# The last projection of a hybrid linear-attention layer: gate folded into the weights, partial products added into the rows, engine order pinned

## The chip, the core and the metric

The kernel runs on one NeuronCore of a Trainium2 chip. Five engines work in parallel, each through its own queue in order: PE (TensorE, matmuls; its weight loads are listed as PEld), DVE (VectorE), ACT (ScalarE), POOL (GpSimd) and SP (SyncE, which here only issues DMAs). An engine waits at the head of its queue until the semaphores that its next instruction names are set, and everything queued behind that instruction waits with it. 16 DMA engines carry the transfers between DRAM and on-chip memory (SBUF). Matmuls write to PSUM, a small accumulation memory.

The metric is the device time of one execution in microseconds, as the median of several runs.

## The reference, cut to what matters

One layer normalises the latent rows, runs two linear-attention mixers over them, merges the two with sigmoid gates, projects with `w_o`, multiplies by a residual gate `gt_x` (one value for each of 1024 columns), adds the input rows and applies a final RMSNorm. The change touches what is computed by these lines:

```
merged = gates[..., :D_MODEL] * jnp.matmul(ya, w_gla_out) + gates[..., D_MODEL:] * jnp.matmul(yb, w_gdn_out)
out_x = jnp.matmul(merged, w_o)                       # 2048 rows x 1024, w_o 1024 x 1024
x = x + (gt_x[:, None, :] * out_x).astype(dtype)
return rmsnorm(x, final_g)                            # x * rsqrt(mean(x*x) + 1e-6) * g, row by row
```

All is float32. The kernel gets that accuracy by splitting each operand into a rounded half (`hi`) and a remainder (`lo`), and multiplying hi by hi, hi by lo and lo by hi.

## The kernel before

Up to about 1770 us of the profile the kernel projects the inputs and runs the two mixers; none of that changes. Then comes its last part, in two stages.

**Merge** (`out_merge`, four calls with g = 0 to 3, each for 512 rows). For each of 8 column tiles j and both mixers i there are 12 matmuls of 128x512 into one PSUM bank (L1597): i = 0 into `pm` (two banks), i = 1 into `pz` for g > 0 (three banks). DVE multiplies each bank by its gate tile `ga` (L1600), adds the two (L1604), and SP writes the sum to the DRAM tensor `d_m` (L1605). Gate tiles are loaded by SP (L1592) into three buffers for i = 0, which come free when the write to `d_m` has landed, and four for i = 1.

**Projection** (`phase_out`, the loop at L1711 to L1776, eight blocks of 256 rows). One level of Strassen's scheme in Winograd's form: a block's input is cut into A11, A12, A21, A22, sums S1 to S4 are formed (`m_sums`, L1643), and seven products p = 0 to 6 (`PRODUCTS`) are taken with seven blocks of weights of 512x512: B11, B21, B22 are cuts of `w_o`, and T1 to T4 are differences of cuts. Each product is 12 matmuls (L1737). Products 0, 2, 4 and 6 add up in one PSUM bank, 1 and 5 in a second, 3 has a third. Partial sums that are needed twice are copied out by ACT (L1742, products 0, 1, 2, 4). DVE or POOL add what is missing (L1751, L1754, L1757), `fin` multiplies by the gate row `gtb` on DVE (L1724), adds into the row tile `x` on POOL (L1725; on DVE at the very end), and ACT squares the result with a row sum (L1726). `flush` takes the reciprocal root on POOL (L1703, then `rsqrt`, L155 and L156), scales the rows on DVE (L1707) and SP writes them out (L1709).

Weights are cut and split by `wo_block`: DMA loads from `w_o` (L1612), differences on DVE (L1624, L1629), `split` (ACT L132 for the rounded half, DVE or POOL L135 for the remainder). B11 and T1 are made ahead of merge 3, T2, B21 and T3 inside it, B22 and T4 inside the first block of the projection. The inputs of a product are split by `m_halves`, through the same two lines, remainders by turns on DVE and POOL.

The order on each engine is chosen by a scheduler from the order of the program and its own estimates of durations; `keep_in_program_order` pins an instruction to its place in program order among those that are pinned. Before, only L1707 in this part is pinned. SP's order comes from the same scheduler.

Of the kernel before, what the change touches and what calls it, by code (L numbers as in the profile page):

```python
# [97 lines left out]
class Build:  # L98
# [1333 lines left out]
    def phase_mix(self):  # L1432
# [4 lines left out]
        self.d_m = dp.tile([NLAT // 2, P, 8, 256], F32, name="dm")  # L1437
        self.d_o = [[dp.tile([P, 512], F32, name=f"do{i}_{l}") for l in range(NLAT)] for i in range(2)]
# [144 lines left out]
    def out_merge(self, g):  # L1583
# [3 lines left out]
        pair = lambda t: t.rearrange("p (e t) -> p e t", e=2)  # L1587
        for j in range(8):
            gs = []
            for i in range(2):  # L1590
# [9 lines left out]
                nc.vector.scalar_tensor_tensor(ga, ga, 1.0, ps, op0=ALU.add, op1=ALU.mult)  # L1600
# [3 lines left out]
            nc.vector.tensor_tensor(gs[0], gs[0], gs[1], op=ALU.add)  # L1604
# [3 lines left out]
    def wo_piece(self, kh, ch, e):  # L1608
        t = self.w_raw().rearrange("p (k n) -> p k n", k=2)
        r0 = (4 * kh + 2 * e) * P  # L1610
        src = self.io["w_o"][0, r0:r0 + 2 * P, 512 * ch:512 * ch + 512]
        self.nc.sync.dma_start(t, src.rearrange("(k p) n -> p k n", p=P))  # L1612
        return t

    def wo_block(self, name, hi, lo):
        nc = self.nc
        for e in range(2):
            ks = slice(2 * e, 2 * e + 2)
            if name[0] == "B":
                x = self.wo_piece(int(name[1]) - 1, int(name[2]) - 1, e)  # L1620
            elif name in ("T1", "T3"):
                a, b = ((0, 1), (0, 0)) if name == "T1" else ((1, 1), (0, 1))
                x, y = self.wo_piece(*a, e), self.wo_piece(*b, e)
                nc.vector.tensor_tensor(x, x, y, op=ALU.subtract)  # L1624
            else:
                o = self.wo["T1" if name == "T2" else "T2"]
                x = self.wo_piece(1, 1 if name == "T2" else 0, e)
                for t in o:
                    nc.vector.tensor_tensor(x, x, t[:, ks].bitcast(F32), op=ALU.subtract)  # L1629
            self.split(hi[:, ks], lo[:, ks], x, lo=self.LO[e])  # L1630
        self.wo[name] = (hi, lo)
# [9 lines left out]
    def m_sum(self, w, nm, a, b, op):  # L1641
        w[nm] = w[b] if nm == "S4" else self.mp.tile([P, 4, P], F32, name="r0" if nm in ("S1", "S3") else "r1", bufs=1)
        self.nc.vector.tensor_tensor(w[nm], w[a], w[b], op=op)  # L1643
# [9 lines left out]
    def m_halves(self, w, p):  # L1653
        hi, lo = (self.mp.tile([P, 4, P], F32R, name=n, bufs=self.NHL) for n in ("hi", "lo"))
        self.split(hi, lo, w[PRODUCTS[p][0]], lo=self.LO[p % 2])
        w[p] = (hi, lo)

    NHL = 4

    def phase_out(self):  # L1660
        nc, io = self.nc, self.io
        with ExitStack() as ctx:
            self.mctx.close()
            fp = self.pool("of", 1, ctx=ctx)
            fg = fp.tile([P, D], F32, name="fgb")
            gtb = fp.tile([P, D], F32, name="gtb")
            nc.sync.dma_start(gtb, self.d_gt[0:1, :].broadcast_to([P, D]))
            nc.sync.dma_start(fg, io["final_g"].unsqueeze(0).broadcast_to([P, D]))
            xp = self.pool("ox", 3, ctx=ctx)
            self.mp = self.pool("om", 1, ctx=ctx)  # L1670
            self.yp = self.pool("oy1", 1, ctx=ctx)
            self.sp = self.pool("og", 4, ctx=ctx)
            self.out_y(1)
            self.wo = {}
            yt = lambda pool, i: [pool.tile([P, 4, 512], F32R, name=f"y{2 * i + x}") for x in range(2)]
            order = [b for g in self.groups for b in g]
            for g in range(1, 4):
                gen = self.out_merge(g)
                if g < 3:
                    y = self.y2  # L1680
                    self.out_y(g + 1)
                    nxt, self.y2 = self.y2, y
                    for _ in gen:
                        pass
                    self.y2 = nxt
                    continue
                self.wo_block("B11", *yt(self.bp, 0))
                self.wo_block("T1", *yt(self.bp, 1))
                for n, _ in enumerate(gen):
                    if n in (3, 7, 11):  # L1690
                        self.wo_block({3: "T2", 7: "B21", 11: "T3"}[n], self.w_blk(), self.w_blk())
            w = self.m_raws(order[0])
            self.m_sums(w, 0)
            for p in range(3):
                self.m_halves(w, p)
            self.m_sums(w, 1)
            pend = []
            pm = self.pool("opp", 3, PSUM, ctx=ctx)

            def flush(parts=1):  # L1700
                while pend:
                    l, x, ss = pend.pop()
                    nc.gpsimd.tensor_tensor(ss[:, 0:1], ss[:, 0:1], ss[:, 1:2], op=ALU.add)  # L1703
                    rs = self.rsqrt(xp, ss[:, 0:1], 1.0 / D, 1, nc.gpsimd)
                    for i in range(parts):
                        cs = slice(i * (D // parts), (i + 1) * (D // parts))
                        self.tc.keep_in_program_order(nc.vector.scalar_tensor_tensor(  # L1707
                            x[:, cs], x[:, cs], rs, fg[:, cs], op0=ALU.mult, op1=ALU.mult))
                        nc.sync.dma_start(self.out[0, l * P:(l + 1) * P, cs], x[:, cs])  # L1709

            for bi, b in enumerate(order):  # L1711
                end = bi + 1 == len(order)
                nw = None if end else self.m_raws(order[bi + 1])
                xs = []
                for i in range(2):
                    x = xp.tile([P, D], F32, name="x")
                    nc.sync.dma_start(x, io["x"][0, (2 * b + i) * P:(2 * b + i + 1) * P, :])
                    xs.append((x, xp.tile([P, 2], F32, name=f"oss{i}")))
                tile_ = lambda: self.sp.tile([P, 512], F32, name="ga")

                def fin(s, src, i, h, last=False):
                    x, ss = xs[i]
                    cs = slice(512 * h, 512 * h + 512)
                    nc.vector.tensor_tensor(s, src, gtb[:, cs], op=ALU.mult)  # L1724
                    (nc.vector if last else nc.gpsimd).tensor_tensor(x[:, cs], x[:, cs], s, op=ALU.add)  # L1725
                    nc.scalar.activation(s, x[:, cs], AF.Square, accum_out=ss[:, h:h + 1])  # L1726

                for p, (_, r) in enumerate(PRODUCTS):
                    if p in (0, 1, 3):
                        ps = pm.tile([P, 512], F32, name="pp") if bi % 2 else self.pv()  # L1730
                        a, c = (ps if p == 0 else a), (ps if p == 1 else None if p == 0 else c)
# [8 lines left out]
                    if p in (0, 1, 2, 4):  # L1740
                        s = tile_()
                        nc.scalar.copy(s, ps)  # L1742
                    if p == 0:
                        s1 = s
                        flush()
                    elif p == 1:
                        s5 = s
                    elif p == 2:
                        s2 = s
                    elif p == 3:  # L1750
# [61 lines left out]
```

## Time and profile before

| | us |
|---|---|
| Median of 3 runs | 2187.87 (2186.38 to 2188.19) |
| The profiled execution | 2195.01 |
| Its span, first to last instruction | 2192.9 |

The page's first part gives each engine's busy time: PE leads with 94% of the span, DVE has 58%, ACT 42%, POOL 41%. That is an average over all stages. The change lies in the last 350 us, so what follows is read from windows of that stretch, from the waits there, from the chain of work that ended last, and from the instructions in order of time. In such a row the first number is the start in us from the start of the span, the second the time in us, then engine, line, operation, output tile, input tiles, and in brackets how long the engine was idle before and what ended the idle time.

### The profile page before, as it was taken

What the parts mean: (1) busy time and instruction counts of PE and PEld (TensorE: products, weight loads), DVE (VectorE), ACT (ScalarE), POOL (GpSimd) and SP (SyncE); (2) the same over time, 40 slices, a digit from 0 to 9 for tenths busy, and PEclk for the clock granted to TensorE, in tenths of its full rate; (3) what the DMA queues carried; (4) which work ended last, traced back from release to release, by engine and by line L of the source; (5) the groups of instructions that cost most, each with busy time, mean ns of one, the idle gap of its engine ahead of it and who ended that gap; (6) DMA issues with size and microseconds to landing.
All of it is one profiled execution on the core that took longest, in us unless ns stands there. A gap on an engine that the chain in (4) does not pass through costs nothing.

```text
span 2192.9 us, 40261 instructions
## 1 busy us (share of the span) xinstructions
PE 2063.7 (94%) x15208; PEld 1690.1 (77%) x15208; DVE 1280.7 (58%) x2188; ACT 926.7 (42%) x2240; POOL 903.7 (41%) x807
## 2 busy tenths in 40 slices
PE   5999999999999999999999999998989889998896
PEld 2688888888888888777777777788878877876675
DVE  3813555567776554555555555666677765467564
ACT  3654255555542223443444443455555551013332
POOL 2410122222320106665666662656566552025554
PEclk7999999999999999999999999999998989999998
DMA  7323122222222224443444444888898877773432
GB/s 278 108 87 115 55 60 64 66 63 61 68 73 75 83 81 144 132 143 118 140 155 136 154 136 150 280 290 304 271 303 278 272 215 243 239 228 130 163 106 87
DMA packets 289758, 337.52 MB, mean 154 GB/s; under 512 B 23208, under 2 KB 215964, under 8 KB 289564
## 3 DMA queue, kind: packets, MB, share of 16 engines
q1 hardware_dynamic: 289564, 334.94, 47.0%
q8 instruction: 120, 1.97, 0.4%
q14 instruction: 74, 0.61, 0.1%
HBM read 216.63 MB, written 118.23 MB: 153 GB/s over the span
## 4 chain that ended last, share of the span: by engine, by line
PE 72%; DVE 8%; DMA 7%; ACT 5%; POOL 4%; issue 3%; SPq 1%; DVEq 0%; POOLq 0%; ACTq 0%
PE pz L371 45%; PE pm L1597 3%; PE pz L1597 2%; PE pp L1737 2%; PE pz L1737 2%; DMA g<-dg 1%; PE pe L936 1%; DMA wr<-in_w_o 1%; PE pl L988 1%; PE pl L995 1%; PE pe L1118 1%; PE pz L1080 1%; PE pl L996 1%; DMA ga<-dgate 1%; POOL x L1725 1%
## 5 line engine op out<-in xcount | busy, mean ns | idle before, releaser
L371 PE MATMUL pz<-hi,wh 128*128 128x512 f32 (+1 forms) x1560 | 621.6, 399 | 0.9 <-DVE hi L134 0.8
L371 PE MATMUL pz<-lo,wh 128*128 128x512 f32 (+1 forms) x1560 | 600.5, 385 | 1.8 <-POOL lo L135 1.8
L371 PE MATMUL pz<-hi,wl 128*128 128x512 f32 (+1 forms) x1520 | 588.6, 387 | 0.0
L371 PEld LDWEIGHTS pz<-lo,wh 128*128 128x128 f32 x1560 | 294.7, 189 | 51.1 <-POOL lo L135 3.6
L371 PEld LDWEIGHTS pz<-hi,wh 128*128 128x128 f32 x1560 | 294.5, 189 | 47.1 <-DVE hi L134 1.6
L371 PEld LDWEIGHTS pz<-hi,wl 128*128 128x128 f32 x1520 | 286.2, 188 | 53.6 <-issue 0.4
L135 POOL TENSOR_TENSOR wl<-w,wh 128x1024 fp32r<-128x1024 f32 x44 | 110.9, 2520 | 435.3 <-ACT wh L132 291.0
L569 DVE SCALAR_TENSOR_TENSOR acc<-zpad,cw,acc 128x1024 f32<-128x1024 f32 x192 | 269.9, 1406 | 6.6
L873 DVE CAST_PREDICATED U<-kit,pl 128x256 f16<-128x256 int32 x216 | 91.1, 431 | 138.2 <-PE pl L996 134.4
L989 ACT CAST ppb<-pl 128x256 f16<-128x256 f32 x216 | 73.5, 373 | 166.8 <-PE pl L988 155.7
L1597 PE MATMUL pm<-y,wb 128*128 128x512 f32 x480 | 119.8, 402 | 8.5 <-DVE ga L1600 6.2
L1216 POOL TENSOR_TENSOR E<-E,ak 128x256 f32<-128x256 f32 x96 | 79.0, 843 | 112.2 <-ACT E L1209 65.2
L1597 PEld LDWEIGHTS pm<-y,wb 128*128 128x128 f32 x480 | 91.9, 193 | 30.7 <-DVE ga L1600 6.0
L135 DVE TENSOR_TENSOR sql<-sq,sqh 128x512 fp32r<-128x512 f32 (+1 forms) x36 | 28.0, 805 | 140.1 <-ACT sqh L132 139.9
L624 POOL TENSOR_TENSOR acc<-acc,sq 128x512 f32<-128x512 f32 x32 | 51.4, 1614 | 137.5 <-ACT sq L623 89.7
L554 ACT COPY zpad<-pz 128x512 f32<-128x512 f32 x48 | 28.2, 587 | 137.6 <-PE pz L371 137.6
L1118 PE MATMUL pe<-wt,gh 128*128 128x256 f32 x264 | 76.2, 316 | 9.4 <-ACT E L1209 4.4
L135 POOL TENSOR_TENSOR y<-wr,y 128x1024 fp32r<-128x1024 f32 x11 | 30.2, 2752 | 120.2 <-ACT y L132 120.2
L132 ACT CAST y<-wr 128x1024 fp32r<-128x1024 f32 x22 | 22.4, 1045 | 130.1 <-PE pm L1597 102.6
L873 DVE CAST_PREDICATED Tm<-kit,pl 128x256 f16<-128x256 int32 x180 | 76.2, 423 | 0.0
L995 PEld LDWEIGHTS <-Tm 128*128 128x128 f16 x864 | 55.1, 98 | 26.4 <-issue 21.9
L132 ACT CAST wh<-w 128x1024 fp32r<-128x1024 f32 x44 | 46.2, 1049 | 68.2 <-PE pz L371 56.0
(329 smaller groups left out, 4474.8 us busy)
## 6 DMA issues: line engine op xcount, KB each, us to landing
dgate<-ob SPq DMA_DIRECT2D x96, 256.0 KB, 2.1
gd<-dgd SPq DMA_DIRECT2D x32, 768.0 KB, 9.0
w<-in_w_in SPq DMA_DIRECT2D x44, 512.0 KB, 3.6
qk<-dqkv SPq DMA_DIRECT2D x32, 512.0 KB, 6.1
ga<-dgate SPq DMA_DIRECT2D x64, 256.0 KB, 3.4
x<-in_x SPq DMA_DIRECT2D x28, 512.0 KB, 5.0
dqkv<-acc SPq DMA_DIRECT2D x192, 64.0 KB, 1.6
dgd<-tm SPq DMA_DIRECT2D x36, 256.0 KB, 3.4
```

Of the source, the lines that this page charges most:

```text
L132: nc.scalar.copy(dst_hi, src)
L135: getattr(nc, lo).tensor_tensor(dst_lo, src, dst_hi.bitcast(F32), op=ALU.subtract)
L371: nc.tensor.matmul(ps[:, 0:n], a[:, kk, :], b[:, kk, :], start=(k == 0), stop=(k == last - 1))
L569: nc.vector.scalar_tensor_tensor(acc, src, wcol, acc, op0=ALU.mult, op1=ALU.add)
L624: nc.gpsimd.tensor_tensor(v, v, r, op=ALU.mult)
L873: self.nc.vector.copy_predicated(out, mv, data)
L989: nc.scalar.copy(ppl, pc.rearrange("p h (j i) -> p h j i", i=m))
L995: nc.tensor.matmul(pu[:, h], Tm[:, h], ppl[:, h], start=True, stop=True)
L1118: self.nc.tensor.matmul(out, g[:, i, ct * P:(ct + 1) * P], self.wt[:, d, cols[0]:cols[1]], start=(j == 0), stop=(j == 1))
L1216: nc.gpsimd.tensor_tensor(E[:, :, li, 1], E[:, :, li, 1], k, op=ALU.mult)
L1597: nc.tensor.matmul(ps, self.wab[j // 2][wi][:, 4 * i + k, (j % 2) * P:(j % 2) * P + P], yy[:, k, :], start=(n == 0), stop=(n == 11))
L1737: nc.tensor.matmul(ps, w[p][u][:, kk, :], self.wo[r][v][:, kk, :], start=(k == 0 and p in (0, 1, 3)), stop=(k == 11), skip_group_check=True)
```

## The change

Five edits, all in the last part.

1. **Weights ahead, with the gate in them.** `w_o` is no longer cut for each block. In merges 1 and 2 a generator `prep(k)` (k = 0 to 3, two in each merge) loads two row tiles of `w_o` of 128x1024, multiplies both by `gtb` on DVE (L1670), forms T1 to T4 by four subtractions of 128x512 on DVE (L1661) and writes seven pieces of 256 KB to seven new DRAM tensors `d_wo`. In merge 3 a generator `blocks()` loads the finished blocks from there (L1693, 512 KB each) and splits them (L1699, L1700).
2. **No copies, no gate multiply.** After each product DVE adds the PSUM bank straight to half a row tile, `x += ps` (L1823). Which half follows from `ACC`; a bank that goes on accumulating is read once for each partial sum. L1742, L1751, L1754, L1757, L1724 and L1725 are gone.
3. **Splits.** The rounded half stays on ACT (`m_hi`, L1632, five buffers, one product further ahead than before), the remainder is always on DVE (`m_lo`, L1637, four buffers).
4. **Square, root and scaling** are placed by hand: the square (L1772) one product behind the addition, the root after products 0 and 6, the two scalings (L1785) after products 1 and 2 of the next block.
5. **Order and buffers.** All DVE, ACT and POOL instructions of this part but those of `split` are pinned; the rows of the next block are loaded from product 3 on; row tiles have four buffers (three before), gate tiles for i = 1 three (four before).

```
+        self.d_wo = {r: dp.tile([P, 4, 512], F32, name=f"dwo{r}") for _, r in PRODUCTS}
...
+        pin = self.tc.keep_in_program_order if g else lambda x: x
...
+            def prep(k):
+                a, b = self.w_raw(), self.w_raw()
+                for t, r in ((a, k), (b, k + 4)):
+                    nc.sync.dma_start(t, io["w_o"][0, r * P:r * P + P, :])
+                yield
+                yield
+                for t in (a, b):
+                    pin(nc.vector.tensor_tensor(t, t, gtb, op=ALU.mult))
+                    yield
+                nc.sync.dma_start(self.d_wo["B11"][:, k], a[:, lo_])
...
+                sub(t1, a[:, hi_], a[:, lo_])
+                nc.sync.dma_start(self.d_wo["T1"][:, k], t1)
...
+            def place(nm, raw, e, dst, eng):
+                hi, lo = self.wo[nm] = dst
+                ks = slice(2 * e, 2 * e + 2)
+                pin(nc.scalar.copy(hi[:, ks], raw[e]))
+                pin(eng.tensor_tensor(lo[:, ks], raw[e], hi[:, ks].bitcast(F32), op=ALU.subtract))
...
+                for _ in gen:
+                    next(work, None)
...
+            ACC = ((0, 0), (1, 1), (0, 1), (0, 0), (1, 1), (0, 1), (1, 0))
...
-                    if p in (0, 1, 2, 4):
-                        s = tile_()
-                        nc.scalar.copy(s, ps)
...
+                    square()
+                    i, h = ACC[p]
+                    x, ss = xs[i]
+                    cs = slice(512 * h, 512 * h + 512)
+                    pin(nc.vector.tensor_tensor(x[:, cs], x[:, cs], ps, op=ALU.add))
+                    if p > 2:
+                        sq.append((x, ss, h))
+                    if p in (0, 6):
+                        root()
+                    if p < 4:
+                        self.m_lo(w, p + 3)
+                    elif nw is not None:
+                        self.m_lo(nw, p - 4)
+                    if nw is not None and p == 3:
+                        self.m_sums(nw, 0)
+                    if p < 3:
+                        self.m_hi(w, p + 4)
+                    elif nw is not None:
+                        self.m_hi(nw, p - 3)
...
+                    if p in (1, 2):
+                        flush()
```

How the instructions move is shown at three places. In these rows `x` is a row tile, `pp` and `pz` are PSUM banks of a product, `lo` and `hi` the two halves of a split, `r` a sum S1 to S4, `wr` a raw load.

ACT in the projection, where one block ends and the next begins. Before:

```order
L1726 ACTIVATE ga,oss_23106<-x 128x512
L132 CAST hi<-r_23262 128x512
L1742 COPY ga<-pp 128x512
L132 CAST hi<-r_23198 128x512
L1742 COPY ga<-pp 128x512
L132 CAST hi<-wr 128x512
L1742 COPY ga<-pp 128x512
```

And now, at the same place:

```order
L1772 ACTIVATE ga,oss<-x 128x512
L1632 CAST hi<-r_23064 128x512
L1772 ACTIVATE ga,oss<-x 128x512
L1632 CAST hi<-wr 128x512
L1772 ACTIVATE ga,oss<-x 128x512
L1632 CAST hi<-r_23135 128x512
L1632 CAST hi<-r_23064 128x512
```

The copies of PSUM banks, which stood behind the previous block's squares, are gone from ACT.

DVE in the projection, about a block's worth of its queue before:

```order
L1707 SCALAR_TENSOR_TENSOR x<-x,rsq,fgb 128x1024 x2
L135 TENSOR_TENSOR lo<-r_23094,hi 128x512
L1643 TENSOR_TENSOR r_23196<-wr 128x512
L1643 TENSOR_TENSOR r_23198<-r_23196,wr 128x512
L135 TENSOR_TENSOR lo<-wr,hi 128x512
L1751 TENSOR_TENSOR ga<-pz,ga 128x512
L135 TENSOR_TENSOR lo<-wr,hi 128x512
L1724 TENSOR_TENSOR ga<-ga,gtb 128x512 x2
L1643 TENSOR_TENSOR r_23262<-wr,r_23198 128x512
L1757 TENSOR_TENSOR ga<-pz,ga 128x512
```

And now, products 0 to 4 of a block:

```order
L1823 TENSOR_TENSOR x<-x,pp 128x512
L1637 TENSOR_TENSOR lo<-wr,hi 128x512
L1823 TENSOR_TENSOR x<-x,pp 128x512
L1637 TENSOR_TENSOR lo<-r_23294,hi 128x512
L1785 SCALAR_TENSOR_TENSOR x<-x,rsq,fgb 128x1024
L1823 TENSOR_TENSOR x<-x,pp 128x512
L1637 TENSOR_TENSOR lo<-r_23223,hi 128x512
L1785 SCALAR_TENSOR_TENSOR x<-x,rsq,fgb 128x1024
L1823 TENSOR_TENSOR x<-x,pp 128x512
L1637 TENSOR_TENSOR lo<-wr,hi 128x512
L1620 TENSOR_TENSOR r_23380<-wr 128x512
L1620 TENSOR_TENSOR r_23382<-r_23380,wr 128x512
```

Each product now has one addition from its bank, one remainder, and at most one larger task on DVE.

SP in merge 2, where before there were only gate loads (`ga<-dgate`), writes of merged tiles (`dm<-ga`) and a few early loads. It now reads:

```order
L1677 DMA dwoT_14758<-r_21920 128x512
L1679 DMA dwoT_14761<-wr 128x512
L1607 DMA dm<-ga 128x2x256
L1682 DMA dwoT_14759<-r_21921 128x512
L1594 DMA ga<-dgate 128x2x256
L1666 DMA wr<-in_w_o 128x1024
L1594 DMA ga<-dgate 128x2x256 x2
L1607 DMA dm<-ga 128x2x256
L1687 DMA dwoT_14763<-r_21980 128x512
L1594 DMA ga<-dgate 128x2x256 x3
L1693 DMA wr<-dwoB_14757 128x1024
```

The writes to `d_wo` (L1672 to L1687) and the loads of `w_o` (L1666) stand between the gate loads that the merge waits for.

More of the change, by code (lines that the diff above doesn't have):

```diff
@@ L1603, in out_merge @@
                     yield
-            nc.vector.tensor_tensor(gs[0], gs[0], gs[1], op=ALU.add)
+            pin(nc.vector.tensor_tensor(gs[0], gs[0], gs[1], op=ALU.add))
             nc.sync.dma_start(self.d_m[bs, :, j, :].rearrange("b p t -> p b t"), pair(gs[0]))
             yield
[L1608 to L1631, printed above, removed]
     def m_raws(self, b):
@@ L1682, in phase_out @@
                     nxt, self.y2 = self.y2, y
[L1683 to L1698, printed above, removed]
+                    work = itertools.chain(prep(2 * g - 2), prep(2 * g - 1))
+                else:
+                    nxt, work = None, blocks()
+                for _ in gen:
+                    next(work, None)
+                for _ in work:
+                    pass
+                self.y2 = nxt
@@ new lines, in phase_out, with square, root @@
+            w = self.m0
+            sq, done, pend = [], [], []
+            def square():
+                for x, ss, h in sq:
+                    junk = self.sp.tile([P, 512], F32, name="ga")
+                    pin(nc.scalar.activation(junk, x[:, 512 * h:512 * h + 512], AF.Square, accum_out=ss[:, h:h + 1]))
+                sq.clear()
+            def root():
+                for l, x, ss in done:
+                    pin(nc.gpsimd.tensor_tensor(ss[:, 0:1], ss[:, 0:1], ss[:, 1:2], op=ALU.add))
+                    pend.append((l, x, self.rsqrt(xp, ss[:, 0:1], 1.0 / D, 1, nc.gpsimd)))
+                done.clear()
@@ L1711, in phase_out @@
+            nxs = load_x(order[0])
             for bi, b in enumerate(order):
                 end = bi + 1 == len(order)
+                xs = nxs
                 nw = None if end else self.m_raws(order[bi + 1])
[L1714 to L1718, printed above, removed]
@@ new lines, in phase_out @@
+                    if nw is not None and p == 3:
[4 more added lines that the diff above has]
+                        self.m_hi(nw, p - 3)
+                    if nw is not None and p == 6:
+                        self.m_sums(nw, 1)
+                    if p in (1, 2):
+                        flush()
+                    if p == 3 and not end:
+                        nxs = load_x(order[bi + 1])
@@ L1775, in phase_out @@
+                    if bi == 0 and p < 4:
+                        if p % 2 == 0:
+                            d = yt(self.yp, 0) if p else wt()
+                        place(("B22", "T4")[p // 2], self.late[p // 2], p % 2, d, nc.gpsimd)
+                    if p == 5:
+                        done.append((2 * b, *xs[0]))
+                    elif p == 6:
+                        done.append((2 * b + 1, *xs[1]))
                 w = nw
+            flush()
+            square()
+            root()
```

159 lines of the change are left out of this document (101 added, 58 removed).

## The prediction

> **What bounds the kernel now.** I read the busy time of the engines in windows first, then PE's waits from 1925 us on, then the chain of work and the instructions in order of time.
>
> ```profile
> 1800.00:1900.00 100.00, 95.36 (x417) 77.27 (x416) 48.86 (x61) 19.87 (x51) 22.63 (x11) 0.98 0.79 253
> 1900.00:2000.00 100.00, 92.83 (x389) 74.72 (x388) 62.93 (x69) 18.12 (x23) 21.18 (x9) 0.97 0.66 203
> 2000.00:2100.00 100.00, 85.74 (x329) 66.32 (x328) 65.14 (x69) 36.04 (x77) 59.33 (x57) 0.91 0.37 131
> 2100.00:2193.00 93.00, 73.32 (x294) 57.45 (x292) 48.85 (x58) 29.50 (x66) 47.04 (x52) 0.90 0.29 103
> ```
>
> Columns: window, length, busy PE, PEld, DVE, ACT, POOL, granted PE clock, share of the DMA engines, GB/s. The merges (to 1979) keep PE busy; the projection, from there on, does not, at a lower clock, and there the DMA engines are idle two thirds of the time. What PE waits for:
>
> ```profile
> PE pp L1737 <- ACT ga L1742: 10.5, 5, 3.2
> PE pz L1737 <- ACT ga L1742: 9.3, 4, 3.2
> PE pz L1737 <- ACT y L132: 3.9, 1, 3.9
> PE pz L1737 <- DVE ga L1600: 2.9, 1, 2.9
> PE pm L1597 <- DVE ga L1600: 2.3, 2, 1.5
> PE pz L1737 <- POOL y L135: 0.7, 1, 0.7
> ```
>
> Total us, times, longest. The rows of L1737 sum to 27.3 us: 19.8 for ACT's copies, 7.5 where merge turns into projection. How large the stage is, and how fast its matmuls can go:
>
> ```profile
> 1979.43 0.63 PE L1737 MATMUL pz<-y,hi 128*128 128x512 f32 x2
> ...
> 2033.76 1.16 PE L1737 MATMUL pp<-y,hi 128*128 128x512 f32 x2 [1.89 <-ACT ga L1742]
> 2034.71 0.63 PE L1737 MATMUL pp<-y,lo 128*128 128x512 f32 x1
> ...
> 2035.99 0.63 PE L1737 MATMUL pp<-y,lo 128*128 128x512 f32 x1
> ...
> 2046.37 0.63 PE L1737 MATMUL pz<-wb,hi 128*128 128x512 f32 x2
> ...
> 2056.17 0.63 PE L1737 MATMUL pz<-wb,hi 128*128 128x512 f32 x2
> ...
> 2181.04 0.39 PE L1737 MATMUL pp<-y,lo 128*128 128x512 f32 x1
> ```
>
> The first row begins the projection, the last ends it: 2181.43 - 1979.43 = 202.0 us. From 2046.37 to 2056.17 lie 14 groups of three matmuls: 0.70 us a group, 2.80 a product, 19.6 a block. 8 blocks are 156.8 us. So 45.2 us are lost: 27.3 in waits, 17.9 in slow matmuls. The rows at 2034.71 and 2035.99 show those: after the wait of 1.89 us a group takes 1.28 us, not 0.70. Why PE waits for a copy of 0.57 us:
>
> ```profile
> 2082.02 1.30 POOL ga L1754
> 2083.34 1.76 DVE ga L1724
> 2086.30 1.10 DVE lo L135
> 2088.09 1.67 POOL x L1725
> 2089.75 0.80 issue
> 2090.78 1.23 POOL x L1725
> 2093.80 7.42 PE pz L1737 x24
> ```
>
> In the chain, product 2 of a block starts (2093.80) when ACT has copied product 0; the copy stands behind the squares of the block before, these behind POOL's additions (L1725), these behind DVE's gate multiply. The waits for `ga` above count nine of these for eight blocks: about one a block.
>
> **The change: the projection.** A bank is now read by one DVE addition. The nearest rows:
>
> ```profile
> L1751 DVE TENSOR_TENSOR ga<-pz,ga 128x512 f32<-128x512 f32 x3 | 2.1, 688 | 1.8 <-PE pz L1737 1.8
> L135 DVE TENSOR_TENSOR lo<-wr,hi 128x512 fp32r<-128x512 f32 x10 | 6.8, 683 | 0.0
> L1643 DVE TENSOR_TENSOR r<-wr,r 128x512 f32<-128x512 f32 x11 | 7.5, 678 | 0.0
> L1707 DVE SCALAR_TENSOR_TENSOR x<-x,rsq,fgb 128x1024 f32<-128x1024 f32 (+1 forms) x17 | 27.3, 1643 | 37.8 <-POOL rsq L156 37.8
> L132 ACT CAST hi<-r 128x512 fp32r<-128x512 f32 x22 | 13.3, 614 | 1.2 <-PE pz L1737 0.8 <-PE pp L1737 0.4
> L1726 ACT ACTIVATE ga<-x 128x512 f32<-128x512 f32 x23 | 14.6, 633 | 57.4 <-POOL x L1725 57.4
> 2184.47 1.28 DVE L1707 SCALAR_TENSOR_TENSOR x<-x,rsq,fgb 128x1024 f32<-128x1024 f32 x1 [2.24 <-POOL rsq L156]
> ```
>
> DVE in a block: 7 additions x 0.69 + 7 remainders x 0.68 + 4 sums x 0.68 + 2 scalings x 1.28 = 14.9 us (15.6 at the mean of 1.64), under 19.6. The fullest products hold 0.69 + 0.68 + 2 x 0.68 = 2.73 or 0.69 + 0.68 + 1.28 = 2.65, under 2.80, and a bank is wanted again only one product later, so DVE may run 2.1 us late before PE feels it. ACT: 7 x 0.61 and 4 squares of 0.82 (0.63 and 0.19 to read the sum) are 7.6. POOL keeps small roots. Each remainder is made two products ahead; the root of a row is asked for at least one product ahead of its scaling; in SP's queue the second half of a block's input, though behind two writes of rows, is issued a whole block ahead. I find no steady wait: 8 x 19.6 = 156.8.
>
> I allow 3.3 us for the first block. The remainder for its product 1 comes after the last merge additions (1.0), POOL's splits of B22 and T4 hold up DVE's sums before product 6 (0.7), and one wait slows the matmuls (three groups x 0.58 = 1.7, rounded down to 1.6). Bounds: 0 to 7.5, today's whole loss at this place.
>
> **The tail.**
>
> ```profile
> 2185.67 0.69 DVE x L1725
> 2186.36 0.02 issue
> ...
> 2188.38 0.75 DVE x L1707
> ```
>
> Today PE's last matmul is followed by 2192.9 - 2181.43 = 11.5 us. The last addition starts only at 2185.67, behind a gate multiply and a scaling; from its end 2.0 us pass to the last scaling, and 4.5 from there to the end. Now the addition starts 0.1 after PE: 0.1 + 0.7 + 2.0 + 4.5 = 7.3; 7.5 with a wait for the other row's scaling. Gain 4.0.
>
> **The merges pay for it.**
>
> ```profile
> DMA packets 16830, 20.32 MB, mean 242 GB/s; under 512 B 1014, under 2 KB 14393, under 8 KB 16825
> q1 hardware_dynamic: 16825, 20.26, 77.3%
> ...
> 1800.00:1810.00 10.00, 10.00 (x46) 8.29 (x45) 3.91 (x6) 7.50 (x36) 5.54 (x4) 1.00 0.94 294
> ...
> 1882.41 0.69 DVE L1600 SCALAR_TENSOR_TENSOR ga<-ga,pm 128x512 f32<-128x512 f32 x1 [2.75 <-DMA ga<-dgate]
> ```
>
> The first two rows are of 1848 to 1932, merges 1 and 2: 242 GB/s at 77.3% share, so 313 at a full one. The third is the highest share of any 10 us window here, 0.94 at 294 GB/s. From SP's order I count in these two merges 27 writes of 0.262 MB (7.08 MB), 6 loads of `w_o` (3.15; two more go ahead of merge 1) and 3 early loads of finished blocks (1.57); 3 row loads and 5 cuts of `w_o` leave them (-4.19). 20.32 + 7.61 = 27.93 MB in 84 us is 332 GB/s, more than the DMA engines give. At 293 (0.94 x 313) they need 95.3 us, 11.3 too many. The last row shows what a late gate does: DVE waits 2.75 us and PE, in this trace, not at all. PE needs the bank of a first product back three products later, 3 x 2.75 = 8.2 us. So of 11.3 us PE sees 3.1. Merge 3 has 11.8 MB up to its last gate load, 40.3 us at 293 against 43.9 of matmuls, and adds nothing. Its 2.3 us of waits (the `pm` row above) also come from late gates and splits, and I take them as replaced: the end without any wait is 1977.1, the forecast 1977.1 + 3.1 + 1.6 for one slow stretch = 1981.8. Bounds: 1977.1 if packets of 2 and 4 KB move faster than the mix, and +20 if the writes that wait for DVE at SP's head leave the DMA engines idle a seventh of the time. I take the middle since 294 was held here.
>
> [...] The trace's best window stays at 294.
>
> DVE's work for `prep`, by the nearest rows:
>
> ```profile
> 1961.47 1.23 DVE L1624 TENSOR_TENSOR wr<-wr 128x1024 f32<-128x1024 f32 x1 [4.02 <-DMA wr<-in_w_o]
> ...
> L135 POOL TENSOR_TENSOR wb<-wr,wb 128x1024 fp32r<-128x1024 f32 x8 | 19.8, 2479 | 35.1 <-ACT wb L132 35.1
> ```
>
> Two multiplies of 1.23 and four differences of 0.68 are 5.2 us a time, 10.4 a merge, beside 17 us of gates in 43.9: hidden. In merge 3 five POOL splits of 2.5 us can each hold up a DVE addition; these were there before too. If this cover fails, a gate comes late and the 8.2 us of slack take it.
>
> **Sum.** 1981.8 + 156.8 + 3.3 + 7.5 = 2149.4, against the span of 2192.9: 43.5 us less. The profiled execution took 2195.01 with 2.1 outside the span, and 7.1 more than the median of 2187.87; I subtract the 43.5 from the median: **2144.4 us**.
>
> **Rivals.**
>
> *The DMA engines bound the merges.* For it: 332 GB/s asked, and SP's queue waits for DVE between gate loads. Against: 8.2 us of slack and 294 GB/s in a row. At +20 us instead of +4.7: 2159.7. Chance 0.17.
>
> *The copy's wait comes back as a DVE wait.* All is pinned, so one late input (a root, a row load, a half of the next input) holds up every addition behind it. For it: the fullest products leave 0.07 us. Against: the slack of 2.1 us and the work ahead. Priced as today's typical wait, 2.0 us and 1.6 of slow matmuls in 7 blocks: +25, 2169.6. Chance 0.13. The change then wouldn't do what it says in the loop, and keep only the transition and the tail.
>
> *Slower.* The DMA engines fall to about 200 GB/s over all three merges, because SP's head waits in turn for DVE, for writes to land and for free buffers. The window of 1900 to 2000 has 203, though it asked for no more. 39.7 MB (27.93 + 11.8) at 200 take 199 us against 128 + 8.2: +62, where my sum has 4.7: +57, 2202. It turns slower than before at 39.7 MB in 128 + 8.2 + 48 = 184 us, 216 GB/s. Chance 0.05.
>
> [...]
>
> **How the numbers follow.** Forecast 0.62, DMA 0.17, DVE wait 0.13, slower 0.05, and 0.03 for a mixture that ends within 0.2% of before (4.4 us, about what a measurement of this kernel can tell from no change). Faster 0.92, same 0.03, slower 0.05. Low end: no loss in the merges (1977.1), none in the first block, which is 8.0 less, and 2.4 for splits that come earlier: 2134. High end: the DVE wait, 2169.6, and 2.4 of DMA lag with it: 2172.
>
> **What would show it.** Right: matmuls of the projection every 0.70 us a group over whole blocks, PE's waits in L1816 under 5 us in sum, some 160 us from its first matmul to its last, granted clock 0.97 or more there; merges 1 and 2 at a DMA share of 0.9 with gates late for DVE (L1602) by several us, PE waiting little; 7 to 8 us after the last matmul. Wrong: PE waiting for L1602 in merge 2 by over 10 us; a wait for L1823 or for L1637 once a block; projection groups slower than 0.70 though nothing waits.

## The result, and the profile after

| | us |
|---|---|
| Before, median of 4 runs | 2187.12 |
| After, median of 4 runs | 2137.86 (2133.87 to 2139.5) |
| After, the profiled execution | 2133.87 |
| Its span | 2132.1 |

The ratio is 0.9777, 95% interval 0.9756 to 0.9798: 49.3 us less, where 43.5 were forecast (2144.4). The time lies inside the range.

The two profiled spans differ by 60.8 us, more than the medians do. Ahead of merge 0 nothing was changed, and yet its first matmul starts at 1783.2 in the trace of before and at 1772.8 in that of after; in the fourteen traces of this study it starts anywhere between 1772.3 and 1784.9. So traces are compared here by stages, each counted from its own first matmul. "Merges" runs from the first matmul of merge 1 into `pz` to the first of the projection, "projection" from there to the end of the last matmul, "tail" from there to the end of the span.

| us | merges | projection | PE's waits in it | slow matmuls in it | tail | all three |
|---|---|---|---|---|---|---|
| before | 131.6 | 202.0 | 27.3 | 17.9 | 11.5 | 345.1 |
| after | 130.35 | 159.5 | 2.3 | 0.4 | 7.5 | 297.4 |

(Slow matmuls: the stage less the waits less 156.8.) These stages give 47.7 of the 49.3 us.

Windows of after, with the columns of the prediction's windows:

```profile
1850.00:1900.00 50.00, 50.00 (x219) 40.72 (x218) 36.38 (x47) 4.20 (x4) 4.90 (x2) 1.00 0.95 321
1900.00:1977.00 77.00, 76.38 (x331) 61.52 (x329) 52.28 (x60) 18.36 (x22) 18.32 (x8) 1.00 0.90 295
...
2007.00:2026.60 19.60, 19.60 (x86) 15.83 (x85) 14.01 (x20) 7.02 (x15) 2.51 (x7) 1.00 0.44 162
```

PE is busy in nearly all of the merges' time, at a granted clock of 1.00. The third row is one block of the projection by itself: PE 19.60 of 19.60 us, DVE 14.01 (14.9 was counted ahead), ACT 7.02 (7.6). The projection's first and last matmul, the piece of the chain that is block 1, and all that PE waits for from the first `pz` matmul of merge 1 to the end:

```profile
1962.30 2.96 PE L1599 MATMUL pz<-y,wb 128*128 128x512 f32 x12
1965.10 0.63 PE L1816 MATMUL pz<-y,hi 128*128 128x512 f32 x2
...
2124.23 0.39 PE L1816 MATMUL pp<-y,lo 128*128 128x512 f32 x1
```

```profile
1987.80 19.56 PE pp L1816 x84
```

```profile
PE pz L1816 <- DVE x L1823: 2.3, 3, 1.1
```

2124.62 - 1965.10 = 159.5 us. Block 1 is 84 matmuls in a row, 19.56 us. None of the six rows of waits in the prediction is left. In their place is one row, three waits in block 0 for a bank that DVE has not yet added to `x`: 0.62 us ahead of product 2, 0.54 ahead of product 4 and 1.10 ahead of product 6. What held DVE up before the last of them (POOL, DVE and PE by time):

```profile
1976.52 5.65 POOL L1700 TENSOR_TENSOR y<-x,y 128x1024 fp32r<-128x1024 f32 x2
...
1979.83 0.68 DVE L1823 TENSOR_TENSOR x<-x,pz 128x512 f32<-128x512 f32 x1
1980.43 2.29 DVE L1637 TENSOR_TENSOR lo<-wr,hi 128x512 fp32r<-128x512 f32 x1
...
1984.80 0.70 PE L1816 MATMUL pz<-y,hi 128*128 128x512 f32 x2 [1.10 <-DVE x L1823]
```

While POOL splits T4, DVE's addition out of PSUM takes its usual 0.68 us, and the remainder, which reads two SBUF tiles, takes 2.29; from 1990 on, behind these splits, remainders take 0.69 on the mean. What causes this in the chip is not shown. The first of the three waits comes before this POOL work; there the addition stands behind the last additions of merge 3 and two sums.

The DMA engines from 1848 to 1932 (the clock times of the prediction's rows), then over just merges 1 and 2 of this trace (1831.95 to 1920.29), and one of the latest gates on DVE:

```profile
DMA packets 18052, 26.40 MB, mean 314 GB/s; under 512 B 1376, under 2 KB 12639, under 8 KB 18048
q1 hardware_dynamic: 18048, 26.35, 94.6%
```

```profile
DMA packets 19755, 27.61 MB, mean 313 GB/s; under 512 B 1410, under 2 KB 14466, under 8 KB 19749
```

```profile
1928.47 0.69 DVE L1602 SCALAR_TENSOR_TENSOR ga<-ga,pz 128x512 f32<-128x512 f32 x1 [2.61 <-DMA ga<-dgate]
```

313 to 314 GB/s, held over 84 and 88 us. Gates come up to 2.6 us late for DVE, and PE sees none of it. The tail:

```profile
2124.66 0.69 DVE L1823 TENSOR_TENSOR x<-x,pp 128x512 f32<-128x512 f32 x1 [2.06 <-PE pp L1816]
...
2127.53 1.42 DVE L1785 SCALAR_TENSOR_TENSOR x<-x,rsq,fgb 128x512 f32<-128x512 f32 x2 [0.99 <-POOL rsq L156]
```

The last addition starts 0.04 us after PE's end; the whole tail is 7.5 us, as worked out.

### The profile page after: what moved, and what is told of

The parts are those of the page before. It is cut to its first block, busy times and chain, and to the rows that moved or that the text cites. A ratio compares the mean times of both kernels' runs of the same rounds, so it can differ in the third digit from the quotient of the medians.

```text
span 2132.1 us, 40259 instructions
## 1 busy us (share of the span) xinstructions
PE 2035.2 (95%) x15208; PEld 1668.2 (78%) x15208; DVE 1285.0 (60%) x2229; ACT 913.8 (43%) x2208; POOL 815.9 (38%) x746
## 3 DMA queue, kind: packets, MB, share of 16 engines
q1 hardware_dynamic: 291868, 344.38, 49.3%
## 4 chain that ended last, share of the span: by engine, by line
PE 74%; issue 6%; DMA 6%; ACT 5%; DVE 4%; POOL 3%; SPq 1%; DVEq 0%; POOLq 0%; ACTq 0%
PE pz L371 48%; PE pm L1599 3%; PE pz L1599 2%; DMA g<-dg 2%; PE pe L1118 2%; PE pe L936 1%; PE pl L995 1%; PE pl L988 1%; DMA ga<-dgate 1%; PE pl L996 1%; PE pz L1080 1%; ACT E L1209 1%; PE pz L1059 1%; DVE ql L1215 1%; PE pp L1816 1%
## 5 line engine op out<-in xcount | busy, mean ns | idle before, releaser
L132 ACT CAST wh<-w 128x1024 fp32r<-128x1024 f32 x44 | 46.2, 1049 | 67.9 <-PE pz L371 56.0
L1209 ACT ACTIVATE E<-pe 128x128 f32<-128x128 f32 x320 | 64.5, 305 | 18.3 <-PE pe L1118 17.7
L1215 DVE TENSOR_TENSOR ql<-E,q 128x256 f32<-128x256 f32 x96 | 63.6, 690 | 12.6 <-ACT E L1206 11.0
```

What stands on the lines that cost most here:

```text
L1209: nc.scalar.activation(E[:, ct, li, x].rearrange("p (j e i) -> p e j i", e=2, i=m), s[:, x * P:(x + 1) * P].rearrange("p (e j i) -> p e j ...
L1215: nc.vector.tensor_tensor(ql[:, li], E[:, :, li, 0], q, op=ALU.mult)
```

## The experiments

All are measured beside the kernel before on the same chip. By the ratios, a distance of 0.001 is 2.2 us; the intervals are 0.002 to 0.004 to each side. Stages come from one profiled execution each.

| us | ratio (interval) | merges | projection | waits in it | tail |
|---|---|---|---|---|---|
| after | 0.9777 (0.9756 to 0.9798) | 130.35 | 159.5 | 2.3 | 7.5 |
| e1 copies back | 0.9804 (0.9781 to 0.9827) | 130.3 | 161.4 | 2.8 | 9.05 |
| e2 gate multiply and POOL back | 0.9827 (0.9808 to 0.9847) | 131.55 | 165.6 | 6.4 | 9.8 |
| e3 no pins | 0.9827 (0.9807 to 0.9847) | 131.0 | 164.9 | 6.1 | 7.4 |
| e4 before, squares later | 0.9922 (0.9903 to 0.9942) | 131.5 | 186.6 | 19.4 | 11.4 |
| e8 before, squares behind copies | 0.9935 (0.9919 to 0.9952) | 130.7 | 189.5 | 19.8 | 11.1 |
| e9 before, ACT in order | 1.0008 (0.999 to 1.0026) | 131.7 | 204.2 | 37.0 | 10.9 |
| e7 weights as before | 0.9889 (0.987 to 0.9908) | 131.8 | 182.5 | 19.4 | 7.5 |
| e10 2.1 MB more | 0.9861 (0.9824 to 0.9897) | 139.2 | 166.1 | 6.8 | 7.4 |
| e5 4.2 MB more | 0.9893 (0.9869 to 0.9916) | 146.1 | 168.35 | 9.5 | 7.4 |
| e6 8.4 MB more | 0.994 (0.9918 to 0.9961) | 157.2 | 166.9 | 8.3 | 7.5 |
| e11 shifted | 0.9761 (0.9721 to 0.98) | 131.7 | 159.05 | 4.1 | 7.5 |
| e12 shifted, splits on DVE | 0.9744 (0.9723 to 0.9764) | 128.25 | 156.7 | 3.7 | 7.5 |

### e1: the copy back between PE and DVE

```
+                    s = self.sp.tile([P, 512], F32, name="ga")
+                    pin(nc.scalar.copy(s, ps))
+                    square()
-                    pin(nc.vector.tensor_tensor(x[:, cs], x[:, cs], ps, op=ALU.add))
+                    pin(nc.vector.tensor_tensor(x[:, cs], x[:, cs], s, op=ALU.add))
```

> The changed kernel with ACT's copy put back between the bank and DVE's addition, all seven times a block, in pinned order with the copy ahead of the square. Theory (the copy was harmful only because it stood behind squares that waited for POOL and DVE): ACT has 7 x 0.57 + 7.6 = 11.6 us of work in a block of 19.6, the copy waits for nothing but PE, so PE's waits in the projection stay under 5 us and the time is that of the changed kernel, 2138, within 5 us. Rival (any copy between PE and DVE costs): about one wait of 2 us and 1.6 us of slow matmuls a block come back, 29 us, 2167.

The projection is 161.4 us, 1.9 longer, the tail 1.6 longer, since a copy now stands in it. One block, in the same columns as above:

```profile
2020.00:2039.60 19.60, 19.60 (x86) 15.83 (x85) 14.05 (x20) 10.19 (x22) 3.60 (x6) 1.00 0.44 161
```

ACT has 3.2 us more in a block, and PE stays full. The stages are 3.5 us longer than after; by the ratio it is 5.9, just over the 5 expected, with intervals that overlap. The theory holds for the waits: seven copies a block, three more than the kernel before had, do not bring its waits back. A copy as such, in the new order, is not what makes PE wait.

### e2: gate multiply and POOL's addition back

```
+                    pin(nc.vector.tensor_tensor(s, ps, fg[:, cs], op=ALU.mult))
+                    pin(nc.gpsimd.tensor_tensor(x[:, cs], x[:, cs], s, op=ALU.add))
-                    pin(nc.vector.tensor_tensor(x[:, cs], x[:, cs], ps, op=ALU.add))
```

> The changed kernel with the gate multiply put back: DVE multiplies the bank into a tile, POOL adds that to the row tile, ACT squares it. It leaves out the multiplication of the weights by the gate and the one by final_g. Theory (what counts is that the bank is read at once by an engine that is not waiting for the chain behind it): DVE's work in a block stays 14.9 us and POOL gets 7 x 1.67 = 11.7 of 19.6, so PE's waits stay under 8 us in the projection and the time is between 2138 and 2148; POOL's additions may hold up DVE's, which is the only way it could rise further. Rival (the chain of gate multiply and POOL addition is itself the cost): 20 us of waits and 14 of slow matmuls return, 2165 or more.

Waits are 6.4 us, under the 8 expected, and nearly all of them in block 0. The ratio is 10.9 us above after's, just over the 10 that were expected at most. One block, and groups of 2016 to 2130 with busy us and mean ns:

```profile
2040.00:2059.60 19.60, 19.45 (x84) 15.41 (x83) 17.63 (x20) 6.47 (x16) 15.03 (x14) 1.00 0.46 159
```

```profile
L1620 DVE TENSOR_TENSOR r<-wr,r 128x512 f32<-128x512 f32 x12 | 14.8, 1236 | 0.2
L1820 DVE TENSOR_TENSOR ga<-pz,fgb 128x512 f32<-128x512 f32 x21 | 14.4, 686 | 5.7 <-PE pz L1812 5.7
```

DVE rises from 14.0 to 17.6 us a block, not because it has more to do (20 tasks in either) but because its tasks between SBUF tiles take longer beside POOL's additions: the sums in the row above 1.24 us on the mean, not 0.69; the multiply out of PSUM keeps its 0.69. So POOL's chain by itself costs some 6 us of the projection here and uses up most of DVE's room. It does not bring back the 45 of before either.

### e3: no pins

```
-            pin = self.tc.keep_in_program_order
+            pin = lambda x: x
```

(the same in `out_merge`, `m_sum`, `m_hi` and `m_lo`; the scaling stays pinned)

> The changed kernel with all its new pins gone (the scaling stays pinned, as before); the scheduler orders DVE, ACT and POOL by its own estimates. Theory (the copies and the gate chain are the gain, the pins only keep an order that a scheduler would find nearly as well): PE's waits in the projection under 12 us, time between 2138 and 2155. Rival (the order by hand is the gain): waits of 20 us and more in the projection with matmuls of 1.28 us a group behind them, 2165 or more.

```profile
1983.32 0.71 PE L1816 MATMUL pz<-y,hi 128*128 128x512 f32 x2 [3.86 <-DVE ga L1602]
1983.87 0.58 PE L1816 MATMUL pz<-y,lo 128*128 128x512 f32 x1
1984.25 1.05 PE L1816 MATMUL pz<-y,hi 128*128 128x512 f32 x2
...
1985.53 1.05 PE L1816 MATMUL pz<-y,hi 128*128 128x512 f32 x2
```

What comes back is one wait where merge turns into projection: a last gate of merge 3 (L1602) is late in DVE's queue, 3.86 us, with groups of 1.28 behind it (1985.53 - 1984.25). From block 1 on PE waits for nothing. The theory holds: the pins are worth 5.4 us of the projection's 42.5, nearly all of it at the transition. By the ratio the distance is 10.9 us, inside the expected range; the stages of the one trace show 6.0 of it, and the rest stays open.

### e4, e8, e9: the kernel before, with ACT's order mended

Three versions, one after the other. In e4 each square comes one product later, behind the copies, and is pinned there:

```
-                    nc.scalar.activation(s, x[:, cs], AF.Square, accum_out=ss[:, h:h + 1])
+                    sq.append((s, x, ss, cs, h))
...
-                        nc.scalar.copy(s, ps)
+                        pin(nc.scalar.copy(s, ps))
+                    if p:
+                        square()
```

> The kernel before with one thing moved: ACT's squares are issued one product later, behind the copies, and pinned there, so that the copies of products 0 and 1 no longer stand behind the last square of the block before; the scaling comes one product later. Theory: of the 19.8 us of waits for the copies at least two thirds go and with them the slow matmuls, 20 to 30 us, so 2157 to 2167. Rival (a full POOL and DVE delay the copies' buffers or the last addition anyway): the waits only change their place, less than 8 us are gained, 2179 or more.

It gains 17 us; waits for copies fall from 19.8 to 11.0, by less than the two thirds expected. A wait that stayed (POOL and ACT by time):

```profile
2091.50 1.67 POOL L1732 TENSOR_TENSOR x<-x,ga 128x512 f32<-128x512 f32 x1 [0.63 <-DVE ga L1731]
...
2093.20 0.63 ACT L1702 ACTIVATE ga<-x 128x512 f32<-128x512 f32 x1 [1.57 <-POOL x L1732]
...
2094.86 0.57 ACT L1749 COPY ga<-pp 128x512 f32<-128x512 f32 x1
```

The copy of product 0 still stands behind a square, now that of product 5, and this still behind POOL. The same order stands ahead of the longer waits, up to 2.53 us. In e8 both last squares of a block stand behind the first two copies of the next:

```
-                    if p:
+                    if p in (1, 5) or end and p == 6:
                         square()
```

> The kernel before with both last squares of a block issued behind the copies of products 0 and 1 of the next block (the run with squares one product later had left the square of product 5 ahead of copy 0, and 11.0 us of waits for copies). Theory: nothing that waits for POOL stands ahead of these copies any more, so waits for copies fall from 19.8 to under 4 us; the transition's 8 us stay; time 2155 to 2163. Rival (the copies stand behind more than the squares: late sums, late row loads, remainders on POOL): 8 us or more of waits remain in the later blocks, under another name too, 2167 or more.

Not the under 4 us expected: 12.7 us of waits for copies, and a time, 2172.86, in the rival's range. Now it is the fourth copy of a block:

```profile
2088.06 1.27 POOL L1732 TENSOR_TENSOR x<-x,ga 128x512 f32<-128x512 f32 x1 [4.48 <-DVE ga L1731]
...
2089.36 0.63 ACT L1702 ACTIVATE ga<-x 128x512 f32<-128x512 f32 x1 [6.02 <-POOL x L1732]
...
2089.98 0.56 ACT L1749 COPY ga<-pz 128x512 f32<-128x512 f32 x1
...
2090.60 1.12 PE L1744 MATMUL pz<-y,hi 128*128 128x512 f32 x2 [2.09 <-ACT ga L1749]
```

This copy is written ahead of the square of product 3, but the casts between weren't pinned, and in ACT's queue the copy came to stand behind that square. In e9 the casts (`split`, L132) are pinned as well.

> The kernel before with all of ACT's work in the projection in one written order: the casts too are pinned now, and each block's squares stand behind its last copy and behind the first two copies of the next block (in the run before this, copy 4 had still slipped behind the square of product 3). Theory: no copy stands behind anything that waits for POOL, so waits for copies fall from 19.8 to under 4 us, the slow matmuls of the later blocks go with them, the transition's 8 us stay; 2155 to 2165. Rival (taking the copies from behind the squares only moves the wait to the late sums, remainders or row loads, because DVE and POOL are late in themselves): PE waits 10 us or more in blocks 1 to 7, 2168 or more.

The theory fell here: 2188.19 us, the time of before. No wait for a copy is left, but from 2030 on (blocks 1 to 7) there are these, 12.5 us with one more row of 0.6, against 18.5 in before:

```profile
PE pp L1749 <- DVE lo L139: 6.8, 4, 2.2
PE pz L1749 <- DVE lo L139: 4.5, 3, 1.5
PE pz L1749 <- POOL lo L139: 0.6, 3, 0.2
```

and in block 0, where the pinned casts of T4's pieces wait for differences and for loads of `w_o`, 16.5 us for `hi` (11.0 the longest). So the rival's numbers came true: with ACT in order, the remainders are what is late. But 24.5 of the 37.0 us of waits are in block 0, where before has 8.8, so the loss in block 0 takes back what the later blocks gain. And every wait for DVE in those later blocks stands behind a pair of scalings, which wait in DVE's queue for POOL's root and which this edit puts one product later:

```profile
2062.73 3.52 DVE L1718 SCALAR_TENSOR_TENSOR x<-x,rsq,fgb 128x1024 f32<-128x1024 f32 x2 [2.56 <-POOL rsq L160]
...
2066.77 0.68 DVE L139 TENSOR_TENSOR lo<-wr,hi 128x512 fp32r<-128x512 f32 x1
2066.90 0.50 PE L1749 MATMUL pz<-wb,lo 128*128 128x512 f32 x1 [1.51 <-DVE lo L139]
```

So ACT's order alone does not save the old loop; e4 is the best of three, and it keeps most of the loss. Whether an order for DVE as well would have saved it was not tried. In the new order one link can come back without the loss: the copies without POOL's chain (e1), or POOL's chain without the copies (e2). No run takes one link out of the kernel before, or puts both back into the changed one.

### e7: the weight blocks as before

`wo_piece` and `wo_block` from the kernel before take the place of `prep` and `blocks`, and the first inputs are made after merge 3.

> The changed kernel with the weight blocks made as before: cut from w_o, differences and splits in merge 3 and in block 0, no way through DRAM; the first inputs are made after merge 3. It leaves out the multiplication by the gate. Theory (the transition's waits came from this work): 7 to 9 us of waits and 3 to 8 of slow matmuls come back in block 0, none in the later blocks; 8 to 16 us over the changed kernel. Rival (the pinned order and the direct additions cleared the transition too, and the work ahead in the merges only adds traffic): under 4 us.

24.5 us by the ratio, where 8 to 16 were expected, and the main loss is not at the transition (4.8 us of wait) but where block 0 turns into block 1:

```profile
2001.34 2.48 DVE L1631 TENSOR_TENSOR wr<-wr,wb 128x1024 f32<-128x1024 f32 x2 [4.01 <-DMA wr<-in_w_o]
...
2005.48 1.93 PE L1756 MATMUL pp<-y,hi 128*128 128x512 f32 x3 [12.96 <-ACT hi L1657]
```

The rounded halves of the next block stand in ACT's queue behind the cast of a piece of T4; ACT waits 7.8 us for DVE's difference for it (L1631), and DVE 4.0 us for the load of `w_o`. After these waits, and one of 1.65 right behind the second, PE waits for nothing more. The kernel before had the same loads and no such wait; that its unpinned order worked around them is argued, not shown. So in these runs the new order needs the weights ahead, through DRAM. What these are worth in the old order by themselves was not tried.

### e10, e5, e6: more transfers in merges 1 and 2

```
+            if g in (1, 2):
+                nc.sync.dma_start(self.dp.tile([P, 512], F32, name=f"dj{g}_{j}"), self.fg[:, :512])
```

This is e5, 16 writes of 0.262 MB. In e6 they are 0.524 MB each, in e10 every second one of e5's.

> The changed kernel with 16 more writes of 0.262 MB (4.2 MB, to tensors that nothing reads) in merges 1 and 2. Theory: these merges have room; at full share the DMA engines move 314 / 0.946 = 332 GB/s, so 26.4 + 4.2 MB need 92.2 us in a stretch of 84, a lag of 8.2, which is just PE's slack of three products less one gate (8.2): PE waits 0 to 3 us in the merges, time 0 to 5 over the changed kernel. Rival (the rate of 293 GB/s of the prediction was right and the merges were at their limit already): 104.4 us, a lag of 20.4, PE waits 12 us or more.

> The same with 16 more writes of 0.524 MB, 8.4 MB. Theory: 34.8 MB at 332 GB/s are 104.8 us, a lag of 20.8, of which the slack hides 8.2: PE waits about 12.6 us in merges 2 and 3, and some slow matmuls follow; 13 to 18 us over the changed kernel. Rival 1 (293 GB/s): a lag of 34.8, waits of 26 us. Rival 2 (transfers are never in the way of the gates): under 3 us.

> The changed kernel with 8 more writes of 0.262 MB (2.1 MB) in merges 1 and 2, half of the smaller dose. Theory, formed from the two doses (+4.2 MB made the merges 15.8 us longer, +8.4 MB 26.9): nothing is left of PE's slack, each added MB goes to PE at 308 GB/s, so merges 7 to 8 us longer. Rival (there is room left, and the loss sets in above a knee between 0 and 4.2 MB): under 3 us.

PE's waits from 1830 on, and after them the DMA engines from 1848 to 1932, first of e5, then of e6, then of e10:

```profile
PE pm L1599 <- DVE ga L1602: 10.9, 7, 4.1
```

```profile
DMA packets 17566, 25.87 MB, mean 308 GB/s; under 512 B 1390, under 2 KB 11533, under 8 KB 17561
```

```profile
PE pm L1599 <- DVE ga L1602: 13.7, 6, 5.4
```

```profile
DMA packets 15247, 26.60 MB, mean 317 GB/s; under 512 B 1233, under 2 KB 9484, under 8 KB 15242
```

```profile
PE pm L1599 <- DVE ga L1602: 5.9, 2, 4.4
PE pz L1818 <- DVE lo L1639: 5.7, 1, 5.7
```

```profile
DMA packets 18128, 26.13 MB, mean 311 GB/s; under 512 B 1413, under 2 KB 12215, under 8 KB 18123
```

My theory for e5 and e6 (332 GB/s and a slack of 8.2 us) fell: by the ratio they are 25 and 36 us over after, where 0 to 5 and 13 to 18 were expected. The waits for gates in the merges, those of `pz` counted in, are 12.0 us in e5, as its rival had it, and 17.7 in e6, between the theory and its rival. With three doses the DMA engines move hardly more than without one, 308 to 317 GB/s, and the merges grow from the first dose on: 2.1 MB add 8.9 us, 4.2 MB 15.8, 8.4 MB 26.9. The theory for e10 (7 to 8 us, no room left) holds within 1 us, and on top of it the first block waits 5.7 us for its inputs, which come from `d_m`. So the kernel after has no reserve for more transfers in its merges.

Whether the limit is the DMA engines' rate or the order in SP's queue, these runs do not separate. In e5 SP itself stands 40.0 us at writes to `d_m` until DVE's sum is there (11.3 in after), with gate loads queued behind, and the share of the DMA engines is 91.1%, not higher than the 94.6 of after.

### e11, e12: tiles 224 bytes further up, and a version that follows from the runs

Comparing stages had shown that a product of the merges does not take the same time everywhere (starts of products in before, after and e11, all in merge 1):

```profile
1861.56 2.91 PE L1597 MATMUL pm<-y,wb 128*128 128x512 f32 x12
1864.31 2.91 PE L1597 MATMUL pz<-y,wb 128*128 128x512 f32 x12
```

```profile
1851.55 2.96 PE L1599 MATMUL pz<-y,wb 128*128 128x512 f32 x12
1854.35 2.96 PE L1599 MATMUL pm<-y,wb 128*128 128x512 f32 x12
```

```profile
1851.54 2.88 PE L1599 MATMUL pm<-y,wb 128*128 128x512 f32 x12
1854.26 2.88 PE L1599 MATMUL pz<-y,wb 128*128 128x512 f32 x12
```

2.75, 2.80 and 2.72 us a product. The edit of e11:

```
+            self.pool("opad", 1, ctx=ctx).tile([P, 56], F32, name="pad")
             self.mp = self.pool("om", 1, ctx=ctx)
```

> The changed kernel with the input halves, sums, row-block halves and gate tiles of this part 224 bytes further up in each partition, nothing else. In the runs so far a product of 12 matmuls takes 2.72 us in merge 2 of every kernel, 2.75 in merges 1 and 3 of the kernel before and 2.80 in those of the changed one, where only the place of the row-block halves differs (offsets of 480, 288 and 256 in 512 bytes). Theory (the place within 512 bytes sets it): 2.72 in merges 1 and 3 as well, and in the projection, whose halves now lie at 480 too; (32 + 56) x 0.08 = 7 us less than the changed kernel. Rival (it is something else): merges 1 and 3 stay at 2.75 to 2.80 and the projection at 2.80, no difference.

The shift does it: 2.72 in all merges, and in the projection groups of 0.68 us where there were 0.70:

```profile
2060.56 0.62 PE L1817 MATMUL pz<-wb,hi 128*128 128x512 f32 x2
...
2061.24 0.62 PE L1817 MATMUL pz<-wb,hi 128*128 128x512 f32 x2
```

```profile
2020.00:2039.04 19.04, 19.04 (x86) 15.77 (x85) 14.03 (x21) 7.03 (x16) 2.48 (x6) 1.00 0.45 166
```

A block takes 19.04 us. The 7 us are nevertheless hardly to be seen in the time (0.9761, inside after's interval): PE reached the late gates of merge 3 (a wait of 3.0) and the held-up additions of block 0 (4.1) sooner. So e12 also moves the weights' remainders from POOL to DVE, and those of B22 and T4 one product later.

```
-                v, g = nc.vector, nc.gpsimd
+                v = g = nc.vector
...
-                        place(("B22", "T4")[p // 2], self.late[p // 2], p % 2, d, nc.gpsimd)
+                        place(("B22", "T4")[p // 3], self.late[p // 3], e, d, nc.vector)
```

> The kernel shifted by 224 bytes, with the remainders of the weight blocks all on DVE (in the run before, every second one on POOL) and those of B22 and T4 one product later. Theory: a split of 2.5 us on POOL holds up a DVE addition or remainder by about 1.6 us (2.18 to 2.88 instead of 0.69), and on DVE it takes 1.22, so DVE gains; in merge 3 the writes to d_m that wait for these additions go out earlier, and in block 0 the additions are on time. The 3.0 us of waits in merge 3 and 4.1 in block 0, with their slow matmuls, go down to under 2 in sum: first merge to end 5 to 8 us shorter, about 2130. Rival (these waits are the gates' and weights' transfers, which are at their limit): no more than 2 us gained, waits of 5 us or more stay.

```profile
PE pz L1817 <- DVE lo L1637: 2.3, 1, 2.3
PE pz L1817 <- ACT hi L1632: 1.4, 1, 1.4
```

The merges have no wait any more and take 128.25 us. In block 0 the additions are on time; 3.7 us are left for the first inputs, more than expected. The three stages are 292.5 us, 5.8 less than e11 and 4.9 less than after. 2133.36 us and 0.9744 make it the fastest kernel of the study; its interval still overlaps after's.

## Why the prediction was right, step by step

**The projection** (forecast 160.1, measured 159.5). The step "I find no steady wait" was right: from block 1 on PE waits for nothing, and DVE's 14.9 us a block were 14.0. The 3.3 us allowed for block 0 were 2.7 (2.3 of waits). The two places named are among the three waits: the last merge additions ahead of the first (0.62 us, where 1.0 was allowed, and for the bank of product 0 instead of a remainder), POOL's splits ahead of product 6 (1.10, where 0.7 was allowed, through an addition that stood behind a remainder and the sums). e12, which moves the splits to DVE and one product later, has none of these waits on `x`. The other 1.6 in that allowance, a slow stretch, wasn't paid; no wait was longer than 1.1 us.

**Why PE waited before** was right as a chain and too narrow as a cause. The prediction reads the copy behind squares, squares behind POOL, POOL behind the gate multiply. e4 and e8 show rows of just this. But e9 shows that with the copies out of that queue the remainders are late instead, behind scalings that wait for POOL's root, and e1 and e2 that in the new order either link can stay if the other is gone. That the loss belonged to the two together, in a loop where ACT, DVE and POOL waited for each other, follows from these runs only in part: the kernel with both links in the new order was not run, nor the old one with one link less.

**The transition** was put among the waits that go. In e3 5.4 us come back without the pins, nearly all of them there; in e7 19.4 us of waits come back, all of them in block 0 and where it ends, without the weights ahead.

**The tail**: 7.5 forecast, 7.5 measured.

**The merges** are the term that was mis-sized: "I take the middle since 294 was held here", for 3.1 us of lag and 1.6 of slow matmuls. Neither was paid. The 2.3 us of waits of before are gone, as forecast, and 1.05 us are lost in a place that the prediction did not have: products of 2.80 us in merges 1 and 3, 2.75 before. So against before the merges are 1.25 us shorter, not 2.4 longer; with the projection's 0.6 that makes 4.2 of the 5.8 us by which the kernel is faster than forecast, and the rest lies within the interval. The count of 27.93 MB was good: 27.61 were moved. Two other things were off. The DMA engines held 313 GB/s, not 293; 317, in e6, was the most that after or a run with a dose held over 84 us of the merges. And the two whole merges were set against 84 us, where they take 88.3; even at 293 GB/s the 27.61 MB need 94.2 us, a lag of 5.9, which the slack of 8.2 would have covered. e10, e5 and e6 show that the limit was near all the same: 2.1 MB more, and what the rival "the DMA engines bound the merges" foretells comes true, 18 us by the ratio. Its chance of 0.17 was, if anything, low for how near it lay.

The rivals "slower" and "the copy's wait comes back as a DVE wait" did not happen; from block 1 on nothing in the trace after points to either.

## What to carry to other kernels

When an engine waits for a short operation, follow the queue of that operation's engine back to where it stops, and count the links: here mending the order of one engine alone gave 17 us at best, while in the new order one link of two could come back and most of the gain stayed. A written order needs the inputs of the pinned engines to be there early: in e7, without the early work, it lost half its gain (24.5 of 49.3 us). And "the transfers fit" has to be tried with a dose: in after PE waits for no gate from the first `pz` matmul of merge 1 on, and 2.1 MB more made the merges 8.9 us longer.

## What the runs showed of the hardware that was not expected

- **Where a tile lay changed PE's pace.** By the compiled programs the row-block halves of merges 1 and 3 begin 288 bytes above a multiple of 512 in before, 256 in after, 480 in e11; those of merge 2 begin at 480 in all. A product of 12 matmuls took 2.75, 2.80, 2.72 and 2.72 us; the granted clock was 1.00 in before and after, and in e12, which has e11's shift. In the projection the groups went from 0.70 to 0.68 us with the same shift. In the merges the operand that moved is the 128x512 one; in the projection's groups with `wb`, which kept its place, it is the 128x128 one. Whether 512 is the right period, and why it happens, was not tried.
- **Not every wait slowed the matmuls.** In the projections of before, after, e1 to e4, e11 and e12 no wait of up to 1.74 us (the longest under 1.8, in e4) was followed by groups of more than 0.82 us. After waits of 1.9 to 2.9 us it went both ways: 1.28 us a group after 1.89 in before, 0.70 after 2.82 in e2, whose row (by time) is

```profile
1993.86 0.70 PE L1812 MATMUL pz<-y,hi 128*128 128x512 f32 x2 [2.82 <-DVE ga L1820]
```

  What decides it is not shown. It is not the length of the wait alone: in e7 a wait of 1.65 us, up to 2009.06, stands 1.9 us behind the one of 12.96 and is followed by groups of 1.28 (2010.50 to 2011.78).
- **Beside POOL's work DVE took longer between SBUF tiles, not out of PSUM.** In e2 a sum between SBUF tiles took 1.24 us on the mean beside POOL's additions and a remainder 0.85, where in after, from 1990 on, they take 0.69; in after a remainder took 2.3 beside POOL's splits. A multiply out of PSUM took 0.69 beside POOL's additions, an addition out of PSUM 0.68 beside its splits.
